# Average pooling by four on one Trainium2 core: sums in two levels of pairs, and the first eight blocks stored singly

## The chip, the cores and the metric

The kernel runs on one core of a Trainium2 chip. Of its engines three matter here: VectorE (DVE in the profile) adds, ScalarE (ACT) multiplies by a constant and issues most of the stores, and SyncE (SP) issues the loads. Sixteen DMA engines move the data between the chip's main memory (HBM) and the core's on-chip memory (SBUF). The metric is the device time of one execution in microseconds; smaller is better. The kernel before takes 1557.08 us, the median of three runs that lie between 1556.96 and 1557.61 us.

## The reference

The input x has the shape (64, 256, 8192) in float32, 537 MB. Every four neighbours along the last axis become their mean, and the groups do not overlap; the output has the shape (64, 256, 2048), 134 MB.

```python
def reference(x, kernel_size, stride):          # 4 and 4
    batch, channels, length = x.shape
    out_len = (length - kernel_size) // stride + 1
    output = np.zeros((batch, channels, out_len), dtype=np.float32)
    for i in range(out_len):
        start = i * stride
        output[:, :, i] = np.mean(x[:, :, start : start + kernel_size], axis=2)
    return output
```

## The kernel before

The input is read as one flat run of numbers and cut into 64 blocks. A block holds 128 partitions of 16384 numbers (`RUN`), so each partition reads 64 KB in one piece and a block is 8.4 MB. Since 16384 is a multiple of 4, no group of four crosses a partition. A block yields 128 x 4096 means, 2.1 MB, in pieces of 16 KB.

Two pools of on-chip buffers carry the work. `xin` has two buffers `xt` for the blocks that come in; `res` has two buffers `r`, each with room for the results of two blocks. The loop takes blocks by pairs. For each block SyncE issues the load (`load`, line 44) and VectorE writes the sums of four into one half of `r` with a single reduction (`sums`, line 48). When both halves are there, ScalarE multiplies the whole buffer by 1/4 in place (`scale`, line 67) and then issues from its own queue one store of both blocks (line 89), which is 4.2 MB.

Block 0 is loaded and summed as two halves (`FIRST`), so that VectorE can begin after the first 4.2 MB. The end has a form of its own: block 62 and the two pieces of block 63 (`LAST`) are summed by `pair_sums`, in two levels. The first level adds neighbours (line 58) and writes the half as many sums over the front of the same input buffer; the second level adds neighbours of those (line 62) into the result buffer. Their results are scaled and stored one by one, and these last stores, with that of blocks 60 and 61, go out from SyncE's queue (lines 98, 101 and 106), behind the last loads.

The order of the work is set by the buffers. With two input buffers, the load of block i + 2 can be issued only when the sum of block i has ended. With two result buffers, the first sum of a pair must wait until the store of the pair two before it has landed. Each engine works through its own instructions in program order; loads and stores sit in two queues, one issued by SyncE and one by ScalarE, and share the same sixteen DMA engines.

Of the kernel before, what the change touches and what calls it, by code (L numbers as in the profile page):

```python
# [1 line left out]

# [4 lines left out]


RUN = 16384

FIRST = (8192, 8192)
LAST = (10240, 6144)


@with_exitstack
def kernel(
    ctx: ExitStack,
    tc: tile.TileContext,
    x: bass.AP,
    kernel_size: bass.AP,  # L20
    stride: bass.AP,
    out: bass.AP,
):
    nc = tc.nc
    K, S = int(kernel_size), int(stride)
    assert K == S == 4
    B, C, L = x.shape
    P = nc.NUM_PARTITIONS
    dt = x.dtype
    M = RUN // K  # L30
    blocks = B * C * L // (P * RUN)
    assert blocks * P * RUN == B * C * L and L % K == 0 and blocks % 2 == 0
    assert sum(FIRST) == sum(LAST) == RUN

    xb = x.rearrange("b c l -> (b c l)").rearrange("(n p m) -> n p m", p=P, m=RUN)
    ob = out.rearrange("b c l -> (b c l)").rearrange("(n p m) -> n p m", p=P, m=M)

    pin = ctx.enter_context(tc.tile_pool(name="xin", bufs=2))
    pout = ctx.enter_context(tc.tile_pool(name="res", bufs=2))

    def load(i, a=0, b=RUN, xt=None):
        if xt is None:
            xt = pin.tile([P, RUN], dt, name="xt")
        nc.sync.dma_start(out=xt[:, a:b], in_=xb[i][:, a:b])  # L44
        return xt

    def sums(o, xt, a=0, b=RUN):
        nc.vector.tensor_reduce(  # L48
            out=o,
            in_=xt[:, a:b].rearrange("p (m k) -> p m k", k=K),  # L50
            axis=mybir.AxisListType.X,
            op=mybir.AluOpType.add,
        )

    def pair_sums(o, xt, a=0, b=RUN):
        v = xt[:, a:b].rearrange("p (m k) -> p m k", k=2)
        h = xt[:, a : (a + b) // 2]
        nc.vector.tensor_tensor(  # L58
            out=h, in0=v[:, :, 0], in1=v[:, :, 1], op=mybir.AluOpType.add
        )  # L60
        w = h.rearrange("p (m k) -> p m k", k=2)
        nc.vector.tensor_tensor(  # L62
            out=o, in0=w[:, :, 0], in1=w[:, :, 1], op=mybir.AluOpType.add
        )

    def scale(o):
        nc.scalar.mul(o, o, 1.0 / K)  # L67

    def edges(cuts):
        at = [sum(cuts[:j]) for j in range(len(cuts) + 1)]  # L70
        return list(zip(at[:-1], at[1:]))

    def both(i):
        return ob[i : i + 2].rearrange("n p m -> p n m")

    for i in range(0, blocks - 2, 2):
        r = pout.tile([P, 2, M], dt, name="r")
        for h in range(2):
            if i + h == 0:
                xt = None  # L80
                for a, b in edges(FIRST):
                    xt = load(0, a, b, xt)
                    sums(r[:, 0, a // K : b // K], xt, a, b)
            else:
                xt = load(i + h)
                sums(r[:, h, :], xt)
        if i < blocks - 4:
            scale(r[:])
            nc.scalar.dma_start(out=both(i), in_=r[:])

    n = blocks - 1
    t = pout.tile([P, 2, M], dt, name="r")
    xt = load(n - 1)
    xl = None
    for a, b in edges(LAST):
        xl = load(n, a, b, xl)
    scale(r[:])
    nc.sync.dma_start(out=both(n - 3), in_=r[:])
    pair_sums(t[:, 0, :], xt)
    scale(t[:, 0, :])  # L100
    nc.sync.dma_start(out=ob[n - 1], in_=t[:, 0, :])
    for a, b in edges(LAST):
        o = t[:, 1, a // K : b // K]
        pair_sums(o, xl, a, b)
        scale(o)
        nc.sync.dma_start(out=ob[n][:, a // K : b // K], in_=o)


# [1 line left out]
_INS = ['x', 'kernel_size', 'stride']  # L110
_OUTS = [((64, 256, 2048), 'float32')]

_NUMBERS = {'kernel_size': 4, 'stride': 4}


# [26 lines left out]
```

## Time and profile before

| What | Value |
|---|---|
| Median of the runs | 1557.08 us |
| Profiled execution | 1556.03 us, its span 1554.3 us |
| VectorE busy | 1094.2 us (70%) in 69 instructions |
| ScalarE busy | 226.6 us (15%) |
| Read and written | 536.87 MB and 134.22 MB |
| Mean rate of the transfers | 432 GB/s |
| Reduction of one block (line 48) | 17.22 us |
| The same block in two levels (lines 58 and 62) | 8.69 us and 4.43 us |
| Scale of two blocks, of one block (line 67) | 7.03 us, 3.62 us |
| Store of two blocks from ScalarE's queue, issue to landing | 49.0 us (median) |
| Load of a block, issue to landing | 31.1 us (median) |

The page lists the busy time of every engine, then the span in 40 slices with a digit for the busy tenths of each, then the transfers. The span is shorter than the profiled execution's time by 1.7 us, which lie around it. A load's time from issue to landing counts its wait in the queue behind the load before it. In lists of instructions the part in brackets is the time for which the engine had been idle, and what ended that.

### The profile page before, as it was taken

To read this page: it belongs to the slowest core of one execution; us is meant where nothing else is said; L and a number is where in the kernel's file an instruction comes from. 1 tells how busy PE (TensorE), PEld (TensorE's weight loads), DVE (VectorE), ACT (ScalarE), POOL (GpSimd) and SP (SyncE) were. 2 spreads that over 40 slices of the span, in tenths; PEclk is the share of its full clock that TensorE was granted. 3 is DMA by queue.
4 is the path that set the end of the run, shared out by engine and by line. 5 is a ranking of instruction groups with operands and counts; after the bars stand their busy time and mean duration, and the time that the engine had idled before them with its cause. 6 is when DMAs were issued, how large, how long until landed. Compare 5 with 4: busy or idle time off the path is not lost.

```text
span 1554.3 us, 402 instructions
## 1 busy us (share of the span) xinstructions
DVE 1094.2 (70%) x69; ACT 226.6 (15%) x35; POOL 0.2 (0%) x4
## 2 busy tenths in 40 slices
DVE  4848767677676776767767667676686766867766
ACT  0110011100111101111011110111101111011111
POOL 0000000000000000000000000000000000000000
DMA  9999999999999999999999999999999999999999
GB/s 420 405 444 432 425 439 431 439 434 423 435 433 434 445 433 433 434 432 427 439 439 432 435 421 435 436 432 439 437 429 428 439 428 443 439 430 437 430 428 400
DMA packets 18371, 671.12 MB, mean 432 GB/s; under 512 B 1600, under 2 KB 1600, under 8 KB 1728
## 3 DMA queue, kind: packets, MB, share of 16 engines
q1 hardware_dynamic: 10208, 545.26, 81.1%
q10 hardware_dynamic: 8160, 125.83, 18.9%
q14 instruction: 3, 0.02, 0.0%
HBM read 536.87 MB, written 134.22 MB: 432 GB/s over the span
## 4 chain that ended last, share of the span: by engine, by line
DMA 64%; DVE 35%; ACT 1%; issue 0%; SPq 0%; DVEq 0%
DMA xt<-in_x_dram 60%; DVE r L48 33%; DMA out_dram<-r 3%; DVE xt L58 1%; DVE r L62 1%; ACT r L67 1%; SPq L44 0%; DVEq L62 0%; DVEq L48 0%; DVEq L58 0%
## 5 line engine op out<-in xcount | busy, mean ns | idle before, releaser
L48 DVE TENSOR_REDUCE r<-xt 128x4096 f32<-128x16384 f32 (+1 forms) x63 | 1067.8, 16949 | 439.1 <-DMA out_dram<-r 226.5
L67 ACT ACTIVATE r<-r 128x8192 f32<-128x8192 f32 (+3 forms) x34 | 225.3, 6628 | 1315.2 <-DVE r L48 1294.0
L58 DVE TENSOR_TENSOR xt<-xt 128x8192 f32<-128x8192 f32 (+2 forms) x3 | 17.5, 5843 | 7.6 <-DMA xt<-in_x_dram 7.6
L62 DVE TENSOR_TENSOR r<-xt 128x4096 f32<-128x4096 f32 (+2 forms) x3 | 9.0, 3003 | 0.2
L67 ACT ACT_TABLE_LOAD x1 | 1.3, 1283 | 0.7 <-PEq L123 0.7
L123 POOL MEMSET const-bfloat16-1.0<- 128x1 bf16 x1 | 0.1, 101 | 0.0
L123 POOL MEMSET const-uint8-127<- 128x1 uint8 x1 | 0.1, 101 | 0.0
L123 POOL MEMSET const-float32-0.0<- 128x1 f32 x1 | 0.1, 98 | 0.2 <-issue 0.2
L123 POOL MEMSET const-float32-1.0<- 128x1 f32 x1 | 0.1, 98 | 0.0
## 6 DMA issues: line engine op xcount, KB each, us to landing
out_dram<-r ACTq DMA_DIRECT2D x30, 4096.0 KB, 49.0
xt<-in_x_dram SPq DMA_DIRECT2D x2, 4096.0 KB, 16.9
xt<-in_x_dram SPq DMA_DIRECT2D x1, 5120.0 KB, 19.6
out_dram<-r SPq DMA_DIRECT2D x1, 4096.0 KB, 29.6
xt<-in_x_dram SPq DMA_DIRECT2D x1, 3072.0 KB, 26.5
out_dram<-r SPq DMA_DIRECT2D x1, 2048.0 KB, 17.0
out_dram<-r SPq DMA_DIRECT2D x1, 1280.0 KB, 13.0
xt<-in_x_dram SPq DMA_DIRECT2D x62, 31.1
```

What stands on the lines that cost most here:

```text
L48: nc.vector.tensor_reduce(out=o, in_=xt[:, a:b].rearrange("p (m k) -> p m k", k=K), axis=mybir.AxisListType.X, op=mybir.AluOpType.add,)
L58: nc.vector.tensor_tensor(out=h, in0=v[:, :, 0], in1=v[:, :, 1], op=mybir.AluOpType.add)
L62: nc.vector.tensor_tensor(out=o, in0=w[:, :, 0], in1=w[:, :, 1], op=mybir.AluOpType.add)
L67: nc.scalar.mul(o, o, 1.0 / K)
L123: nc = _bacc.Bacc("TRN2", target_bir_lowering=False, num_devices=1)
```

## The change

There are three parts. First, every block is summed in two levels of pairs: the reduction is gone, and what was `pair_sums` is now `sums`. Second, block 0 is loaded whole, as all others are. Third, for the first eight blocks (`SINGLES`) each block's half of `r` is scaled and stored by itself, with a store of 2.1 MB from ScalarE's queue as soon as it is summed; from block 8 on, two blocks are scaled and stored together as before. The end of the kernel is the same, except for the name of the function that sums.

```diff
-FIRST = (8192, 8192)
+SINGLES = 8
 LAST = (10240, 6144)
...
     def sums(o, xt, a=0, b=RUN):
-        nc.vector.tensor_reduce(
-            out=o,
-            in_=xt[:, a:b].rearrange("p (m k) -> p m k", k=K),
-            axis=mybir.AxisListType.X,
-            op=mybir.AluOpType.add,
-        )
-
-    def pair_sums(o, xt, a=0, b=RUN):
         v = xt[:, a:b].rearrange("p (m k) -> p m k", k=2)
         h = xt[:, a : (a + b) // 2]
         nc.vector.tensor_tensor(
             out=h, in0=v[:, :, 0], in1=v[:, :, 1], op=mybir.AluOpType.add
         )
...
     for i in range(0, blocks - 2, 2):
         r = pout.tile([P, 2, M], dt, name="r")
         for h in range(2):
-            if i + h == 0:
-                xt = None
-                for a, b in edges(FIRST):
-                    xt = load(0, a, b, xt)
-                    sums(r[:, 0, a // K : b // K], xt, a, b)
-            else:
-                xt = load(i + h)
-                sums(r[:, h, :], xt)
-        if i < blocks - 4:
+            xt = load(i + h)
+            sums(r[:, h, :], xt)
+            if i < SINGLES:
+                scale(r[:, h, :])
+                nc.scalar.dma_start(out=ob[i + h], in_=r[:, h, :])
+        if SINGLES <= i < blocks - 4:
             scale(r[:])
             nc.scalar.dma_start(out=both(i), in_=r[:])
...
-    pair_sums(t[:, 0, :], xt)
+    sums(t[:, 0, :], xt)
...
-        pair_sums(o, xl, a, b)
+        sums(o, xl, a, b)
```

More of the change, by code (lines that the diff above doesn't have):

```diff
@@ L32 @@
     assert blocks * P * RUN == B * C * L and L % K == 0 and blocks % 2 == 0
-    assert sum(FIRST) == sum(LAST) == RUN
+    assert sum(LAST) == RUN
     xb = x.rearrange("b c l -> (b c l)").rearrange("(n p m) -> n p m", p=P, m=RUN)
```

## The prediction

> **What bounds the kernel now.** I read the page's 40 slices first, then its DMA table, then the sum of the windows, then the chain, then the timeline at the two ends.
>
> ```profile
> span 1554.3 us, 402 instructions
> DVE 1094.2 (70%) x69; ACT 226.6 (15%) x35; POOL 0.2 (0%) x4
> DVE  4848767677676776767767667676686766867766
> ...
> DMA  9999999999999999999999999999999999999999
> GB/s 420 405 444 432 425 439 431 439 434 423 435 433 434 445 433 433 434 432 427 439 439 432 435 421 435 436 432 439 437 429 428 439 428 443 439 430 437 430 428 400
> ...
> HBM read 536.87 MB, written 134.22 MB: 432 GB/s over the span
> ```
>
> All 40 DMA digits are 9, while VectorE is at six or seven tenths: the transfers bound the kernel and VectorE has slack in every slice. Only slices 2 (405) and 40 (400) lie well under the rest. The next view is the windows; the columns after the stretch are its length, the busy time of three engines, the clock, the DMA share and GB/s.
>
> ```profile
> 1.50:59.00 57.50, 34.28 (x3) 0.51 (x1) 0.00 (x0) 1.00 1.02 438
> 59.00:64.00 5.00, 2.87 (x2) 4.66 (x1) 0.00 (x0) 1.00 0.90 354
> 64.00:1514.00 1450.00, 1030.64 (x60) 213.24 (x31) 0.00 (x0) 1.00 1.00 433
> 1516.00:1541.00 25.00, 24.84 (x6) 5.95 (x2) 0.00 (x0) 1.00 0.99 425
> ```
>
> From 64 us to 1514 us the 16 DMA engines are full. The one hole is 59 to 64 us, with a share of 0.90. Short windows are lumpy, since transfers of 64 KB pieces start together, so this row is good to some tenths of a microsecond. Why the hole is there is in the timeline (start, duration, instruction, idle time before it):
>
> ```profile
> 13.03 8.69 DVE L48 TENSOR_REDUCE r<-xt 128x2048 f32<-128x8192 f32 x1 [13.03 <-DMA xt<-in_x_dram]
> 22.73 8.69 DVE L48 TENSOR_REDUCE r<-xt 128x2048 f32<-128x8192 f32 x1 [1.01 <-DMA xt<-in_x_dram]
> 42.09 17.22 DVE L48 TENSOR_REDUCE r<-xt 128x4096 f32<-128x16384 f32 x1 [10.67 <-DMA xt<-in_x_dram]
> ...
> 61.43 17.22 DVE L48 TENSOR_REDUCE r<-xt 128x4096 f32<-128x16384 f32 x1 [2.13 <-DMA xt<-in_x_dram]
> 66.40 0.42 ACTq L89 DMA_DIRECT2D out_dram<-r  x1
> 86.00 17.22 DVE L48 TENSOR_REDUCE r<-xt 128x4096 f32<-128x16384 f32 x1 [7.35 <-DMA xt<-in_x_dram]
> ...
> 1441.29 17.22 DVE L48 TENSOR_REDUCE r<-xt 128x4096 f32<-128x16384 f32 x1 [6.12 <-DMA xt<-in_x_dram]
> ...
> 1489.65 17.22 DVE L48 TENSOR_REDUCE r<-xt 128x4096 f32<-128x16384 f32 x1 [6.12 <-DMA xt<-in_x_dram]
> ...
> 1514.51 8.69 DVE L58 TENSOR_TENSOR xt<-xt 128x8192 f32<-128x8192 f32 x1 [7.64 <-DMA xt<-in_x_dram]
> 1523.29 4.43 DVE L62 TENSOR_TENSOR r<-xt 128x4096 f32<-128x4096 f32 x1
> ...
> 1538.37 4.54 SPq L106 DMA_DIRECT2D out_dram<-r  x2
> ```
>
> A load can only be issued once the sum two blocks earlier has freed its buffer. Load 3 is issued when the sum of block 1 ends (42.09 + 17.22 = 59.3) and load 2 lands at 61.4: a cover of 2.1 us, too little to start the next transfer without a hole, and no store exists yet to fill it (the first is issued at 66.40). Later the cover is the 6.12 us that VectorE idles for its load, stores are always in flight, and two blocks take 1489.65 - 1441.29 = 48.36 us.
>
> So the price of the start can be read. Load 2 takes 61.43 - 42.09 = 19.34 us alone. From its landing to that of load 3 pass 85.98 - 61.43 = 24.55 us; 19.34 of that is load 3 and about 3.5 the store beside it (in flight for about 17.7 us, at a fifth of the bytes as in the steady pairs: 4.19 of 20.97 MB). **About 1.7 us are lost there**, an estimate: 0.5 by the window (0.10 of 5 us) is the hole, the other 1.2 falls after it, where the first store runs beside loads.
>
> The chain of waits gives VectorE's sums 33% of the span. It runs through them only because a load's time from issue to landing (31.1 us) includes the wait behind the load before it; it does not show that a faster sum moves the end.
>
> **The change, part by part.**
>
> *Sums in two levels.* Reduction of a block: 17.22 us. The pair form is in the tail: 8.69 + 4.43 = 13.1 us. Sixty-two blocks (the first as two halves) save 4.1 us each, VectorE falls from 1094 to about 840 us busy. On the path: nothing in the steady part, as transfers hide it; cover rises there from 6.1 to about 10.2 us. The new in-place first level writes the input buffer, so the next load waits for both adds; that is in the 13.1. In a pair's first block only the second add writes r and must wait for the store of the pair four blocks earlier; the first add no longer does (226.5 us of VectorE idleness now stand behind that wait). Were the second add to start at that landing, as the sum at 1466.31 does now, the load behind it would be issued at 1470.7 instead of 1483.56, against a landing at 1489.65.
>
> *First load whole.* VectorE starts at about 22.7 instead of 13.0 and ends block 0 at 35.9 instead of 31.4. Load 2 is issued then, 6.2 us before load 1 lands at 42.1: hidden by load 1, which without that cover would cost whatever exceeds about 2 us. One load issue fewer (about 0.4 us of SyncE) is off the path. Load 3 is issued at 42.1 + 13.2 = 55.3, 6 us before load 2 lands. **The hole of 0.5 us goes.** Bounds: 0, and the whole 1.7. I take 0.5, the row of the hole itself.
>
> *Eight single stores.* Scales of 128x4096 cost 3.62 us (the tail's row) against 7.03 for two blocks, 0.2 us more per pair on ScalarE, which works 15%. Four more store issues at 0.4 us lie on ScalarE's queue; behind each stands only the next scale, 24 us off. The first store leaves at 35.9 + 3.6 = 39.5 instead of 66.4. The transfers carry the same bytes in the same 16 KB rows; being full, they only carry some earlier. A single takes half of the pair's 49.0 us, so one store is nearly always open and the last single lands near 235; the first pair store is issued after block 9, near 256. For some 20 us only loads run, 19.3 us apart, against sums of 13.1: cover 6.2, no hole. The 1.2 us seen when the first store joined the loads has no cause in the page. Bounds: it is not paid at all (-1.2), paid once as before (0), or paid again when stores resume near 256 (+1.2). I take 0: an interruption of stores is not a first store, and no slice after the second sags.
>
> The Trainium skill speaks against this part: "DMA: Bandwidth & Descriptors", section "Anatomy of one DMA", gives each transfer about 2.0 us of fixed cost, and "SBUF — State Buffer", section "The DMA setup-cost knee", asks for the largest single transfer. Four stores more and one load less would be an estimated 6 us by those pages, 1562.6 in all. The trace disagrees for queued transfers: 100 are issued, 200 us by the rule, yet the share is 1.00 over 1450 us.
>
> *Tail.* Its instructions and order do not change. Load 62 lands at 1514.4; adds and scales take 28 us to the last store issue (1542.5), which lands 10.7 us later. Slice 40's 400 is that last landing and the start-up of 1.6 us has its like in slice 1; both stay. Were load 62 to land 0.5 us earlier, the transfers behind it move with it.
>
> **Sum.** Profiled execution: 1556.03 (span 1554.3 and 1.7 around it) - 0.5 = 1555.5. The runs' median is 1.05 above that execution, so the forecast for a median is 1557.08 - 0.5 = **1556.6**.
>
> **Rivals.**
>
> *A. Only the hole goes:* 1556.6, the forecast.
>
> *B. The whole start loss goes:* earlier, smaller stores meet loads without the 1.2 us. For it: the loss followed a hole that is gone. Against: a first store is still there. 1557.1 - 1.7 = 1555.4.
>
> *C. Stores resuming near 256 us pay 1.2 again:* 1557.8.
>
> *D. Slower: the adds slow the transfers.* Pair sums write three times as much on chip as a reduction (8192 + 4096 elements per row against 4096) while transfers write the same memory. For it: the tail window, full of pair sums, has 425 GB/s against 433. At face value, 1.8% over the 54% of the time that VectorE would be adding (13.1 of 24.2 us) is 1.0%, 15 us: 1572. Against: that window holds smaller transfers and its share is 0.99. It decides from a mean rate of 0.9 GB/s under the present one, 3.1 us.
>
> *E. Faster: VectorE sets the pace,* as the chain suggests: 4.1 us for each of its 31 sums, 127 us, 1430. Against: DMA digits of 9 throughout; 671 MB do not fit.
>
> **How the numbers follow.** Chances: A 0.66, B 0.12, C 0.13, D 0.04, the rule of a fixed cost per transfer 0.02, E 0.01, something unseen 0.02. The difference that a measurement of this kernel can tell is taken as 0.2%, 3.1 us. A, B and C are all within it: same 0.91. Slower: D, the rule and half of the unseen, with a little for a case C that is larger, 0.07; faster: 0.02. The range takes in B and C with the runs' own spread (0.1 below, 0.5 above the median): 1555.1 to 1558.1.
>
> **What would show it.** Right: VectorE near 840 us; no wait for a load before 61 us shorter than 5 us; a share near 1.00 from 59 to 64; slices after the second unchanged near 434; landings 24.2 us apart from the third block on; the last store landing some half microsecond earlier. B: blocks 2 and 3 landing exactly 24.2 us apart. C: a sag in slice 7 (about 233 to 272 us). D: every slice below its present value. Wrong: a hole in DMA anywhere after 64 us, or VectorE waiting for stores long enough that SyncE issues a load after the one before has landed.

## The result, and the profile after

The changed kernel takes 1554.53 us (median of 20 runs, 1554.33 to 1556.09); the kernel before took 1557.12 us in the same study (20 runs, 1556.86 to 1557.61). The ratio is 0.9985, with a 95% interval of 0.9978 to 0.9991. The medians lie 2.6 us or 0.17% apart, inside the 0.2% that the forecast called "same", but below its range (1555.1 to 1558.1), and five times the 0.5 us that it expected. The profiled execution after took 1554.40 us with a span of 1552.6 us; that of before had 1556.03 us, so the two profiles differ by 1.6 us and the medians by 2.6.

The page of the changed kernel: the busy times, the slices of VectorE and DMA, and the rates.

```profile
span 1552.6 us, 471 instructions
DVE 839.7 (54%) x130; ACT 227.4 (15%) x39; POOL 0.2 (0%) x4
DVE  3646556546465464654646546455464554645646
...
DMA  9999999999999999999999999999999999999999
GB/s 417 420 434 438 439 439 439 412 445 444 413 433 435 443 438 439 432 424 429 439 438 433 437 434 419 439 432 438 439 419 434 434 437 439 441 423 442 422 440 400
```

VectorE fell from 1094.2 to 839.7 us, as worked out (840), and the time hardly moved: transfers still fill all 40 slices. What moved is slice 2, from 405 to 420 GB/s. Single slices elsewhere wander by some 20 GB/s in both profiles (slice 8 has 412 here, the two behind it 445 and 444), so they are read in longer windows below. The timeline of the start, where the first stores and covers lie:

```profile
35.91 3.62 ACT L59 ACTIVATE r<-r 128x4096 f32<-128x4096 f32 x1 [33.91 <-DVE r L54]
39.56 0.39 ACTq L75 DMA_DIRECT2D out_dram<-r  x1
42.06 8.69 DVE L50 TENSOR_TENSOR xt<-xt 128x8192 f32<-128x8192 f32 x1 [6.18 <-DMA xt<-in_x_dram]
50.79 4.42 DVE L54 TENSOR_TENSOR r<-xt 128x4096 f32<-128x4096 f32 x1
55.25 3.62 ACT L59 ACTIVATE r<-r 128x4096 f32<-128x4096 f32 x1 [15.71 <-DVE r L54]
58.89 0.34 ACTq L75 DMA_DIRECT2D out_dram<-r  x1
66.44 8.69 DVE L50 TENSOR_TENSOR xt<-xt 128x8192 f32<-128x8192 f32 x1 [11.23 <-DMA xt<-in_x_dram]
...
90.66 8.69 DVE L50 TENSOR_TENSOR xt<-xt 128x8192 f32<-128x8192 f32 x1 [11.07 <-DMA xt<-in_x_dram]
...
255.10 8.70 DVE L50 TENSOR_TENSOR xt<-xt 128x8192 f32<-128x8192 f32 x1 [6.17 <-DMA xt<-in_x_dram]
256.02 0.39 ACTq L78 DMA_DIRECT2D out_dram<-r  x1
```

The idle time in brackets is the cover, the time by which the next load was issued before the last one landed. It is 6.18, 11.23, 11.07 and 6.17 us (the last at the switch to stores of two blocks), where the kernel before had 2.13 with no store open. Loads 2 and 3 land 90.66 - 66.44 = 24.2 us apart, as in the steady part of the kernel before (48.36 us for two). The waits of the changed kernel hold no line for VectorE waiting on a store any more; its whole wait is for loads:

```profile
ACT r L59 <- DVE r L54: 1313.0, 38, 44.8
DVE xt L50 <- DMA xt<-in_x_dram: 696.1, 63, 22.7
```

The windows that had the hole (length, three engines' busy time, clock, DMA share, GB/s):

```profile
59.00:64.00 5.00, 0.00 (x0) 0.00 (x0) 0.00 (x0) 1.00 1.17 505
64.00:1514.00 1450.00, 787.96 (x121) 211.48 (x33) 0.00 (x0) 1.00 1.00 434
```

A window counts a piece of a transfer where it starts, so short windows are lumpy; the share of 1.17 comes from that. The hole is gone, and the long middle stands at 434 GB/s against 433 before.

### The profile page after: what moved, and what is told of

The parts are those of the page before. It is cut to its first block, busy times and chain, and to the rows that moved or that the text cites. A ratio compares the mean times of both kernels' runs of the same rounds, so it can differ in the third digit from the quotient of the medians.

```text
span 1552.6 us, 471 instructions
## 1 busy us (share of the span) xinstructions
DVE 839.7 (54%) x130; ACT 227.4 (15%) x39; POOL 0.2 (0%) x4
## 4 chain that ended last, share of the span: by engine, by line
DMA 71%; DVE 28%; issue 0%; ACT 0%; DVEq 0%
DMA xt<-in_x_dram 71%; DVE xt L50 18%; DVE r L54 9%; ACT r L59 0%; DVEq L54 0%
## 5 line engine op out<-in xcount | busy, mean ns | idle before, releaser
L50 DVE TENSOR_TENSOR xt<-xt 128x8192 f32<-128x8192 f32 (+1 forms) x65 | 556.5, 8561 | 696.1 <-DMA xt<-in_x_dram 696.1
L54 DVE TENSOR_TENSOR r<-xt 128x4096 f32<-128x4096 f32 (+1 forms) x65 | 283.4, 4360 | 3.9
```

Of the source, the lines that this page charges most:

```text
L50: nc.vector.tensor_tensor(out=h, in0=v[:, :, 0], in1=v[:, :, 1], op=mybir.AluOpType.add)
L54: nc.vector.tensor_tensor(out=o, in0=w[:, :, 0], in1=w[:, :, 1], op=mybir.AluOpType.add)
```

## The experiments

The theories: H, the hole and what follows it cost all that the change won; S, the hole costs 0.5 us and the rest is the price of a first large store that joins loads; A, the faster adds win it all along the run. Times are medians of 11 runs (20 for the changed kernel, 4 for the slow block), beside runs of the kernel before whose median was 1556.98 to 1557.21 us in every study.

**Two blocks in pairs.** The kernel before, with two-level sums for blocks 0 and 1 alone.

```diff
-                    sums(r[:, 0, a // K : b // K], xt, a, b)
+                    pair_sums(r[:, 0, a // K : b // K], xt, a, b)
...
-                sums(r[:, h, :], xt)
+                (pair_sums if i + h == 1 else sums)(r[:, h, :], xt)
```

> The kernel before, with only blocks 0 and 1 summed in two levels of pairs; the first load in halves, all stores of two blocks. The sum of block 1 should end near 55.3 instead of 59.3 us, so load 3 is issued 6 us before load 2 lands and the hole of the DMA engines at 59 to 64 us is gone, while the first store is still one of 4.2 MB, issued near 62 us. Theory H (the hole and its restart cost all that the change won): 1554.5 us, as the changed kernel. Theory S (the hole costs its 0.5 us, and the rest is the price of a first large store joining loads, which singles avoid): 1556.6 us. Theory A (the faster adds all along win it): within 0.3 us of the kernel before.

Measured: 1554.92 us (1554.75 to 1555.26), ratio 0.9986 (0.9977 to 0.9995). Two faster sums out of 64 bring 2.25 of the 2.6 us, with a first store that is still a large one. Theory A falls: the other sixty sums, the whole first load and the singles together bring some 0.3 us. The timeline of this kernel, with load 2 landing and the first store:

```profile
61.24 17.22 DVE L48 TENSOR_REDUCE r<-xt 128x4096 f32<-128x16384 f32 x1 [6.20 <-DMA xt<-in_x_dram]
62.13 0.41 ACTq L89 DMA_DIRECT2D out_dram<-r  x1
```

**Singles with reductions.** The kernel before, with the first eight blocks stored singly.

```diff
+            if i < SINGLES:
+                scale(r[:, h, :])
+                nc.scalar.dma_start(out=ob[i + h], in_=r[:, h, :])
-        if i < blocks - 4:
+        if SINGLES <= i < blocks - 4:
```

> The kernel before, with only the first eight blocks' means stored singly; reductions everywhere but in the tail, first load in halves. The first store is issued near 35 us, so load 2 shares the engines with it and lands near 66 us; load 3 is issued at 59.3 us with a cover of some 6 us, and the hole goes in this way too. Theories H and S: 1554.5 us. Theory A: within 0.3 us of the kernel before.

Measured: 1557.56 us (1556.69 to 1557.89), ratio 1.0003 (0.9994 to 1.0011): nothing won. H and S both expected 1554.5. The start did get its cover (block 2 lands at 66.96, 5.72 us after the sum before it ended), but the trace shows the same small cover at the switch to stores of two blocks, where only loads run and land 19.6 us apart. The timeline of this kernel there:

```profile
236.09 17.22 DVE L49 TENSOR_REDUCE r<-xt 128x4096 f32<-128x16384 f32 x1 [6.89 <-DMA xt<-in_x_dram]
...
255.72 17.22 DVE L49 TENSOR_REDUCE r<-xt 128x4096 f32<-128x16384 f32 x1 [2.40 <-DMA xt<-in_x_dram]
260.41 0.39 ACTq L93 DMA_DIRECT2D out_dram<-r  x1
```

**Pairs at the switch.** The same kernel with two-level sums for blocks 8 to 13.

```diff
-                sums(r[:, h, :], xt)
+                (pair_sums if 8 <= i + h < 14 else sums)(r[:, h, :], xt)
```

> The run with eight single stores and reductions (1557.56 us), with blocks 8 to 13 summed in two levels of pairs. That run's trace loses as much between 230 and 330 us as at the start: after the last single store only loads run, 19.3 us apart, and reductions of 17.2 us leave a cover of 2.1 us, as at the start. With sums of 13.1 us there the cover is 6 us. Theory H (a hole where no store is open is the price, wherever it stands): 1556.0 us. If the singles or the reductions lose the time elsewhere: 1557.5 us.

Measured: 1554.90 us (1554.66 to 1555.18). The cover at the switch is now 6.18 us, and 2.7 us are won, more than the 1.6 expected: a small cover with no store open costs as much at 255 us as at 60. The pieces of the transfers tell the same: from 260 to 284 us the run with reductions moved 401 GB/s at a share of 0.97, which is 413 at full share, and this one 408 at 0.94, which is 434. The timeline of this kernel:

```profile
236.38 8.69 DVE L59 TENSOR_TENSOR xt<-xt 128x8192 f32<-128x8192 f32 x1 [10.89 <-DMA xt<-in_x_dram]
...
255.71 8.69 DVE L59 TENSOR_TENSOR xt<-xt 128x8192 f32<-128x8192 f32 x1 [6.18 <-DMA xt<-in_x_dram]
```

**No singles.** The changed kernel with `SINGLES = 0`.

> The changed kernel without the single stores: all stores are of two blocks, the first issued near 62 us; adds in two levels, first load whole. The hole is gone. Theory H: 1554.5 us. Theory S: 1556.6 us. Theory A: 1554.5 us.

Measured: 1554.79 us (1554.64 to 1556.52), 2.4 us faster than before. Singles are worth at most some 0.3 us beside this, about as much as the medians of the kernel before differ between studies (1556.98 to 1557.21); theory S falls, since the first store here is a large one.

**A quarter more on block 1.** The run without singles, with one added reduction (`reduce` is the reduction of the kernel before; its output is overwritten).

```diff
+            if i + h == 1:
+                reduce(r[:, h, : 1024], xt, 0, 4096)
             sums(r[:, h, :], xt)
```

> The run without single stores (two-level sums, first load whole, all stores of two blocks: 1554.79 us), with one more reduction over a quarter of block 1 ahead of its sum; its output is overwritten by the sum. The sum of block 1 then ends some 4.4 us later, near 59.4 us, as in the kernel before, with a cover of about 2 us for load 3, and nothing else moves. Theory H (the hole and what follows it cost all that the change won): 1557.2 us. Theory S (the hole costs its 0.5 us): 1555.3 us.

Measured: 1557.52 us (1557.09 to 1558.01). One added instruction of 4.42 us, in block 1 alone, gives back the whole gain and a little more: 2.7 us. This is theory H (1557.2) and not S (1555.3). The landing of load 2 in the run without singles, and then in this one:

```profile
61.23 8.69 DVE L50 TENSOR_TENSOR xt<-xt 128x8192 f32<-128x8192 f32 x1 [6.19 <-DMA xt<-in_x_dram]
```

```profile
61.48 8.69 DVE L50 TENSOR_TENSOR xt<-xt 128x8192 f32<-128x8192 f32 x1 [1.89 <-DMA xt<-in_x_dram]
```

Load 2 lands within 0.25 us of the same moment, and the cover behind it fell from 6.19 to 1.89 us. One more thing moved, against the expectation: the first store is issued at 66.69 instead of 62.13 us. That the loss belongs to the cover and not to this store is shown by the run with only the first load whole, below.

**Half of block 1 more.** The same with `reduce(r[:, h, : 2048], xt, 0, 8192)`.

> The same with one more reduction over half of block 1, 8.7 us: its sum ends near 63.8 us, 2.6 us after load 2 lands; the hole is 4.3 us longer than with the quarter. If the loss is the length of the hole and a fixed price for the restart: 4.3 us above the run with the quarter, 1561.5 us by theory H and 1559.6 us by theory S. If a stopped stream costs one fixed price however long it stops: within 1 us of the run with the quarter.

Measured: 1560.06 us (1559.82 to 1561.0), 2.5 us above the quarter for a sum that ends 4.2 us later (63.77 against 59.59). Neither line of the expectation fits (4.3 and under 1), though the time lies near that of theory S for this run. The loss grows with the stop, but not one to one; the table of landings in the next section shows why.

**Whole first load alone.** The kernel before with `FIRST = (16384,)`.

> The kernel before, with only the first load whole. The reduction of block 0 ends near 39.95 us and load 2 is issued then, 2.1 us before load 1 lands; load 3 as before. Two holes of the same kind instead of one, each with a cover of 2.1 us. Theory H (each hole with its restart costs about 2.6 us): 1559.7 us. Theory S (a hole costs its 0.5 us): 1557.6 us. Theory A: 1557.1 us.

Measured: 1557.19 us (1556.85 to 1557.57), ratio 1.0001. Two holes were expected and there is one: the cover of 2.09 us behind block 0 delays load 2, which lands at 63.18 instead of 61.43, and that delay is the cover for load 3. The run also shows a small cover by itself, as no store has been issued yet: load 2 takes 63.18 - 41.96 = 21.2 us, where it took 61.43 - 42.09 = 19.3 in the kernel before. The timeline of this kernel:

```profile
41.96 17.22 DVE L48 TENSOR_REDUCE r<-xt 128x4096 f32<-128x16384 f32 x1 [2.09 <-DMA xt<-in_x_dram]
59.21 7.03 ACT L67 ACTIVATE r<-r 128x8192 f32<-128x8192 f32 x1 [57.20 <-DVE r L48]
63.18 17.22 DVE L48 TENSOR_REDUCE r<-xt 128x4096 f32<-128x16384 f32 x1 [4.00 <-DMA xt<-in_x_dram]
66.27 0.41 ACTq L89 DMA_DIRECT2D out_dram<-r  x1
```

**Late sums in the middle of the run.** Three kernels from the changed one, each with an added reduction ahead of a single block's sum: all of block 31, half of block 30, three quarters of block 31. The first:

```diff
+            if i + h == 31:
+                reduce(r[:, h, :], xt)
             sums(r[:, h, :], xt)
```

> The changed kernel with block 31 reduced once more ahead of its two-level sum, 17.2 us (output overwritten by the sum). Its cover for the next load falls from 11 us to -6 us in the middle of the run, where a store of two blocks is open. Theory H with the rider that an open store fills the hole: within 0.3 us of the changed kernel, 1554.5 us. If every stop of the loads costs: 6 to 8 us more, 1561 us.

Measured: 1575.08 us (1573.16 to 1576.76), 20.5 us slower, where 0 or 6 to 8 was expected. Two things were wrong. In the trace the first add of block 32 runs ahead of the second add of block 31, so load 33 was issued at 802.5 us instead of 794 (an estimate: 763.59 + 17.22 + 8.69 + 4.43). And no store was open: a store of two blocks takes as long as two loads, so it had just ended with load 32. In the windows nothing starts from 785 to 800:

```profile
785.00:790.00 5.00, 5.00 (x2) 0.00 (x0) 0.00 (x0) 1.00 0.00 0
790.00:795.00 5.00, 5.00 (x1) 0.00 (x0) 0.00 (x0) 1.00 0.00 0
795.00:800.00 5.00, 5.00 (x2) 0.00 (x0) 0.00 (x0) 1.00 0.00 0
```

The other two, in which the order of the adds is that of the blocks, ask whether an open store matters:

> The changed kernel with one more reduction over half of block 30 (8.7 us, output overwritten) ahead of its sum. It writes r and so waits for the store of blocks 26 and 27, which lands near 743 us; the sum of block 30 then ends near 765 us, load 32 can start near 767 us and load 31 lands near 763: no load for some 3 us. The store of blocks 28 and 29 is then half done, with some 2 MB left, 5 us of work for the engines alone. Theory H with its rider (an open store fills the stop, and the loads catch up later): 1554.5 us, within 0.5. If every stop of the loads costs its length: 1558 us.

> The changed kernel with one more reduction over three quarters of block 31 (12.9 us, output overwritten). Its sum ends near 790 us, load 33 can start near 791.5, and load 32 lands near 787, where the store of blocks 28 and 29 lands too, since a store of two blocks and two loads take the same time; the next store waits for block 31 itself. No transfer is open for some 4.6 us. Theory H with its rider: the hole and a price of 1 to 2 us for the restart, 1560 to 1561 us. If only the start of the kernel is sensitive: 1554.5 us.

Measured: 1554.52 us (1554.4 to 1555.12) with block 30 late, and 1560.39 us (1560.13 to 1561.63) with block 31 late. For block 30 the store it waits for landed earlier than expected, so the loads did not stop; the cover fell to 2.25 us, which is the size that cost 2.7 us at the start, and cost nothing here with a store half done. With block 31 late both streams ended and the price is 5.9 us. Theory H with its rider expected both times (1554.5, and 1560 to 1561). The timeline for block 30 late, then the timeline and the windows for block 31 late:

```profile
736.35 0.38 ACTq L88 DMA_DIRECT2D out_dram<-r  x1
...
763.86 8.69 DVE L50 TENSOR_TENSOR xt<-xt 128x8192 f32<-128x8192 f32 x1 [2.25 <-DMA xt<-in_x_dram]
```

```profile
785.92 4.42 DVE L54 TENSOR_TENSOR r<-xt 128x4096 f32<-128x4096 f32 x1
790.26 8.68 DVE L50 TENSOR_TENSOR xt<-xt 128x8192 f32<-128x8192 f32 x1
...
797.44 0.38 ACTq L88 DMA_DIRECT2D out_dram<-r  x1
```

```profile
785.00:790.00 5.00, 4.97 (x2) 0.00 (x0) 0.00 (x0) 1.00 0.00 0
```

**First load in halves.** The changed kernel with the second part of the change undone.

```diff
+            if i + h == 0:
+                xt = None
+                for a, b in edges(FIRST):
+                    xt = load(0, a, b, xt)
+                    sums(r[:, 0, a // K : b // K], xt, a, b)
+            else:
+                xt = load(i + h)
+                sums(r[:, h, :], xt)
-            xt = load(i + h)
-            sums(r[:, h, :], xt)
```

> The changed kernel with the first load in halves again: only the second part of the change undone. Block 0 is done near 29.3 us instead of 35.9, its store leaves near 33 us. The cover for load 2 rises from 6 to 12 us. Theory H: no hole with or without, so within 0.3 us of the changed kernel, 1554.5 us. If the first packets are better small: up to 0.3 us faster; if an earlier store next to loads costs what the run with singles and reductions showed at 47 to 57 us (0.9 us): 1555.2 us.

Measured: 1555.59 us (1554.87 to 1556.1), 1.06 us slower, where theory H expected no difference; the value written down for an earlier store beside loads was 1555.2. Two more kernels took apart the halves and the moment at which the first store leaves: halves, with an added reduction of 6.5 us so that the store leaves at 39.60 instead of 32.91; and the changed kernel with two multiplications by 1.0 ahead of the first store, so that it leaves at 46.95 instead of 39.56.

```diff
+                    if a:
+                        reduce(r[:, 0, a // K : (a + 6144) // K], xt, a, a + 6144)
                     sums(r[:, 0, a // K : b // K], xt, a, b)
```

```diff
                 scale(r[:, h, :])
+                if i + h == 0:
+                    for _ in range(2):
+                        nc.scalar.mul(r[:, h, :], r[:, h, :], 1.0)
```

> The run with the first load in halves (1555.59 us), with one more reduction over three quarters of the second half of block 0 (6.5 us, output overwritten), so that block 0 is done near 35.8 us and its store leaves near 39.5 us, as in the changed kernel. Theory J (the loss depends on the moment at which the first store joins: in the middle of load 1 it costs about 1 us, at the boundary of loads 1 and 2 little): 1554.6 us. Theory P (the halved load itself costs): 1555.6 us.

> The changed kernel with two more multiplications by 1.0 of block 0's results on ScalarE ahead of their store, 7.2 us, so that it leaves near 46.8 us and joins near 49 us, in the middle of load 2 instead of at its start; no load moves. Theory J: about 1 us slower, 1555.5 us. Theory P: 1554.5 us.

Measured: 1554.74 us (1554.37 to 1554.92) and 1554.85 us (1554.76 to 1555.2). The halves cost at most 0.2 us by themselves, and the earlier end of block 0 the other 0.85: theory J in the first run. Two things move with that end, though, the first store (32.91 to 39.60 us) and the issue of load 2 (29.25 to 35.95), and these runs don't part them. In the second run only the store moves, and the middle of load 2 costs 0.3 us instead of the 1 us that J expected. So it is not the middle of a load as such; why block 0 ready at 29 us costs more than at 36, with a store at 40 or 47, stays open.

**More and fewer singles.** The changed kernel with `SINGLES = 60` and with `SINGLES = 2`.

> The changed kernel with blocks 0 to 59 stored singly instead of 0 to 7. If the stores' size matters only where the first ones join: within 0.2 us of the changed kernel, 1554.5 us. If the switch near 256 us costs something there: up to 0.5 us faster. If each further transfer has a price of its own on the engines: 26 more at up to 2 us each, up to 1606 us.

> The changed kernel with two single stores (blocks 0 and 1) instead of eight; the switch to stores of two blocks then comes near 110 us. If only the first store's moment and size matter: 1554.5 us within 0.2. If the loads need to settle beside single stores before large ones: toward the run without singles, 1554.8 us.

Measured: 1555.65 us (1555.36 to 1555.99) with sixty, 1.1 us slower; 1554.73 us (1554.63 to 1555.35) with two, 0.2 slower. Twenty-six more transfers cost far less than 2 us each. Eight has the lowest median of the four counts tried (0, 2, 8, 60), though 0, 2 and 8 lie within 0.3 us of each other, and no kernel tried is faster than the changed one, beyond the 0.01 us of the run with block 30 late.

**Before, once more.** The kernel before, unchanged, for a second profile.

> The kernel before, unchanged, for a second profile. If the earlier profiled execution was a mild one: a time near 1557.1 us, and between 59 and 90 us a loss some 1 us larger than in the earlier profile. If the difference lies elsewhere: the same first 90 us and about 1 us more in the rest.

Measured: 1556.77 us in its profiled execution, 0.74 above the first profile. Up to 125 us both traces carry 423 GB/s, so the mean rate shows no larger loss between 59 and 90 us. The difference of the times is at the very end. The windows of the last microseconds, first of the earlier profile, then of this one:

```profile
1551.00:1552.00 1.00, 0.00 (x0) 0.00 (x0) 0.00 (x0) 1.00 0.90 375
1552.00:1553.00 1.00, 0.00 (x0) 0.00 (x0) 0.00 (x0) 1.00 0.24 98
1553.00:1554.00 1.00, 0.00 (x0) 0.00 (x0) 0.00 (x0) 1.00 0.00 0
```

```profile
1551.00:1552.00 1.00, 0.00 (x0) 0.00 (x0) 0.00 (x0) 1.00 0.85 354
1552.00:1553.00 1.00, 0.00 (x0) 0.00 (x0) 0.00 (x0) 1.00 0.28 117
1553.00:1554.00 1.00, 0.00 (x0) 0.00 (x0) 0.00 (x0) 1.00 0.09 37
```

In the earlier profile nothing starts after 1553 us; in this one a remnant of 9% of the engines' capacity still does. The landings below show that this unevenness does begin where it was expected, at the load behind the small cover.

## Why the prediction was wrong

The frame was right: transfers bound the kernel, VectorE's 254 us less are hidden, eight single stores in place of four of two blocks cost nothing, and nearly all of the gain lies at the start. The direction was right too.

**The step that failed is "The hole of 0.5 us goes".** The term was mis-sized: the quarter-more run against the run without singles prices it at 1557.52 - 1554.79 = 2.7 us, outside the bounds of 0 to 1.7 that the step gave. The 0.5 was read from a row that doesn't measure the hole: the same row, 59 to 64 us, has a share of 0.90 in the first profile of the kernel before and 0.96 in the second, 0.97 without singles, where the cover is 6.19 us, and 1.17 after. Beyond that it failed in three ways.

First, I split the loss at the start, 1.7 us, into a hole (0.5 by the window) and 1.2 for a first store that joins loads, and kept the second. The runs without the hole but with a large first store (1554.92 and 1554.79) show that most of this goes with the hole. The price of the small cover is not only the time in which engines idle; transfers after it are slow. This is read from two columns of a window, the rate divided by the share. From 64 to 88 us, in the kernel before, with the quarter more, without singles, and after:

```profile
64.00:88.00 24.00, 16.65 (x2) 2.37 (x1) 0.00 (x0) 1.00 0.95 392
```

```profile
64.00:88.00 24.00, 10.98 (x3) 2.65 (x1) 0.00 (x0) 1.00 0.99 409
```

```profile
64.00:88.00 24.00, 13.51 (x3) 0.00 (x0) 0.00 (x0) 1.00 1.01 423
```

```profile
64.00:88.00 24.00, 13.12 (x2) 3.62 (x1) 0.00 (x0) 1.00 1.01 437
```

At full share that is 392 / 0.95 = 413, 409 / 0.99 = 413, 423 / 1.01 = 419 and 437 / 1.01 = 433 GB/s; the steady part has 433. Busy engines were 4.6% slow after the small cover, 3.3% where only a large first store joined, and not at all in the changed kernel, where the store had joined 20 us earlier; when it joined, from 36 to 60 us, that kernel had 456 / 1.06 = 430. The slow ones are the loads: their pieces of 64 KB took 2.58 us on average in the first of these windows and 2.42 in the last. A busy share near 1 hid this from me; slow packets count as busy. Rival B, which let the whole 1.7 go, had 0.12. Its reason ("the loss followed a hole that is gone") was right, and so was its sign, blocks 2 and 3 landing 24.2 us apart; its means were not, as the runs with a large first store show that earlier, smaller stores are hardly needed. Between the two profiles its size fits: 1556.03 - 1554.40 = 1.6 us.

Second, the forecast carried the profile's price over to the median by adding a constant 1.05 us. That execution was a rare one: the runs of the kernel before lie between 1555.99 and 1558.22 us in all studies, and a single one of them is faster. Part of the typical loss was not in the trace that I priced. The second profile shows one place for it, the uneven end. The quarter-more kernel, whose profiled execution took 1557.96 us, has it as well, and the changed kernel's does not; the last windows of the one and of the other:

```profile
1552.00:1553.00 1.00, 0.00 (x0) 0.00 (x0) 0.00 (x0) 1.00 0.46 193
1553.00:1554.00 1.00, 0.00 (x0) 0.00 (x0) 0.00 (x0) 1.00 0.21 86
```

```profile
1550.00:1551.00 1.00, 0.00 (x0) 0.00 (x0) 0.00 (x0) 1.00 0.53 221
1551.00:1552.00 1.00, 0.00 (x0) 0.00 (x0) 0.00 (x0) 1.00 0.02 6
```

Where this unevenness comes from is in the kept traces, though the views above print only the last landing of a transfer: the traces hold sixteen landing times for each. The spread is the time from the first to the last of the sixteen (all in microseconds):

| Kernel | Cover | Spread of the load ahead of it | Spread of the next load | Last store: mean landing | Last store: last landing | Its spread |
|---|---|---|---|---|---|---|
| Before, first profile | 2.13 | 0.66 | 1.22 | 1552.59 | 1553.26 | 1.30 |
| Before, second profile | 2.13 | 0.42 | 1.88 | 1552.65 | 1553.99 | 2.19 |
| A quarter more | 1.89 | 0.55 | 2.52 | 1553.17 | 1555.26 | 2.96 |
| Singles with reductions, at the switch | 2.40 | 0.43 | 2.21 | 1553.14 | 1554.67 | 2.26 |
| Whole first load alone, load 2 | 2.09 | 0.51 | 1.73 | 1553.05 | 1554.78 | 2.42 |
| No singles | 6.19 | 0.49 | 0.31 | 1551.36 | 1552.05 | 0.94 |
| Pairs at the switch | 6.18 | 0.43 | 0.46 | 1551.66 | 1552.40 | 1.04 |
| After | 11.23 | 0.51 | 0.54 | 1551.02 | 1551.75 | 0.99 |
| Half more (load issued 2.4 late) | none | 0.57 | 0.53 | 1556.49 | 1557.14 | 0.92 |

Behind each cover of about 2 us the sixteen parts of the next load land further apart, and a spread is still there at the end, where the last part sets the time. So the price has two parts. From before to after, by the first profile, the mean landing moved by 1.57 us and the spread hardly counted. In the quarter more against no singles the mean moved by 1.81 us and the last part fell another 1.40 us behind the mean, 3.2 us in all, as the profiled times differ (1557.96 and 1554.74). The second profile of the kernel before differs from the first by 0.06 us in the mean and 0.67 in the last part behind it: that is the mild execution. Half more has the longer stop and no unevenness, so against the quarter its mean is 3.3 us later and 1.4 us of that come back (1559.84 against 1557.96 in the profiled executions).

Three things stay open. A small cover is not the only source of a spread: near the first single store the parts of a load land 1.66 us apart in the run with the first load in halves, 1.34 and 1.38 in the two kernels after it, with 1.61, 1.03 and 0.90 at their ends, and the changed kernel's own spread grows from 0.4 us at 545 us to the 0.99 of its end. That each part is the share of one DMA engine is likely from the number sixteen, but no row names the engine. And no run shows why a short cover makes the parts uneven, when a full stop leaves them even although its transfers are slow too (half more, from 64 to 88 us: 393 / 0.97 = 405 GB/s).

Third, "Bounds: 0, and the whole 1.7" took the one trace's whole start loss for the most that could be won, so the low end of the range came from the same mild execution. (The terms named for the range, 0.1 below rival B and 0.5 above rival C, give 1555.3 to 1558.3; the range on record lies 0.2 lower, without a reason. The measured time lies below both.)

**The other steps.** The cover ahead of load 1's landing was right to 0.1 us (block 0 ends at 35.9, load 1 lands at 42.06, the cover is 6.18), and so was that at the switch, 6.17. The one ahead of load 2's landing was costed at 6 us and is 11.23, since the first store runs beside load 2. Rival C (stores that resume pay again) did not happen in the changed kernel: its windows from 230 to 260 and from 260 to 330 us have 437 and 432 GB/s, and the spread of its loads stays under 0.5 us there. Yet "an interruption of stores is not a first store" was too weak a reason: with reductions the switch costs 2.7 us. It is the faster adds that keep the cover there. Costing the whole first load at nothing holds by itself (1557.19), but in the changed kernel it is worth 1.06 us, as it puts off the end of block 0. The eight singles were costed at 0 and bring at most 0.3 us over none. The wait for stores of 226.5 us went entirely, as the second add comes after the store has landed; it was off the path. Rival D (adds slow the transfers) and the rule of a fixed cost per transfer are excluded by 434 GB/s in the middle and by the time itself. Of that rule, "DMA: Bandwidth & Descriptors" of the Trainium skill, section "Anatomy of one DMA", gives the 2.0 us for transfers that GpSimd issues, while SyncE and ScalarE issue all of these; "SBUF — State Buffer" of the Trainium skill, section "The DMA setup-cost knee", states it for every transfer, and these runs disagree: the sixty singles, 26 transfers more than eight, cost 1.1 us in all. Rival E, with 1430 us, never stood.

## What to carry to other kernels

In a kernel bound by transfers, look for stretches in which only one stream is open, at the start and at every change in the stores' pattern, and read the cover there: 6 us was enough and 2 us cost 2.7 us, while with a second stream open 2 us cost nothing in the one run that tried it. Read the rate divided by the share as well as the share, and price a loss from runs or from several profiles, since one profiled execution may be a mild one. Where transfers end unevenly, ask how far apart the parts of one transfer land, and from which transfer on. An instruction added to one block is a cheap way to price a cover.

## What the runs showed that was not expected

- A load issued 1.9 to 2.4 us before the stream runs dry costs about 2.7 us in all (at 61 us and again at 255 us), several times the hole that the windows show: transfers after it run up to 4.6% slow for some 24 us, and the parts of each transfer land 1.2 to 2.5 us apart from there on, instead of 0.3 to 0.5. A stop longer by 4.2 us added 2.5.
- The parts of the last store land 2.19 us apart in one execution and 1.30 in another of the same kernel, while their mean differs by 0.06 us (1556.77 against 1556.03 us).
- Block 0 ready some 7 us earlier, and with it the first store of 2 MB (32.91 against 39.60 us) and load 2's issue, costs 0.85 us without any hole; why is open.
- Storing all blocks but the last four singly costs 1.1 us against eight singles. Its last store's parts land 1.89 us apart, against 0.99, with a mean 0.3 us later; the spread grows from 1.02 to 1.88 us only between the last two loads, at 1525 and 1533 us.
